# Strassen-Winograd weight sums made by accumulating transfers, with the signs of the products changed

## The chip, the cores and the metric

The kernel runs on one core of a Trainium2 chip. The metric is device time in microseconds of one execution. TensorE (PE) does the matmuls, VectorE (DVE), ScalarE (ACT) and GpSimd (POOL) the elementwise work; SyncE (SP) only issues transfers, and 16 DMA engines carry them.

## The reference

The model is an encoder of depth 2 over 1024 rows of width 1024, in float32. Layer 0 mixes by a Fourier transform and neighbourhood attention, layer 1 by a gated short convolution; after that each layer has a cross-attention into 256 memory rows and a gated feed-forward part:

```python
def conv_ffn(h, w_up, conv_w, conv_b, w_down):
    z = h @ w_up
    u = z[..., :D_FF]
    g = dwconv3_centred(z[..., D_FF:], conv_w) + conv_b
    return (jax.nn.gelu(g, approximate=False) * u) @ w_down

def short_gated_conv_mixer(h, w_in, conv_w, w_out):
    z = h @ w_in
    gate_b = z[..., :D_MODEL]
    gate_c = z[..., D_MODEL:2 * D_MODEL]
    u = z[..., 2 * D_MODEL:]
    return (gate_b * dwconv3_centred(gate_c * u, conv_w)) @ w_out
```

D_FF is 2048, so `w_up` is 1024 by 4096 and `w_down` 2048 by 1024. The change concerns only these weight matrices: `w_up` and `w_down` of both layers, and `w_in` and `w_out` of the gated convolution.

## The kernel before

Activations lie transposed in SBUF, with features in the partitions and the 1024 rows in the free dimension. A float32 matmul is done as three matmuls of halves (`mm3`, L223 to L227): every operand is split into a rounded part *hi* (ACT, L220) and the rest *lo* (DVE, L221; in some other stages POOL), and PE adds hi·hi, hi·lo and lo·hi in PSUM.

The big projections use the Strassen-Winograd scheme: each 2x2 block product takes seven products p1 to p7 of a sum of weight blocks with a sum of activation blocks in place of eight. The weights are handled in *groups*. A group holds four quarters a11, a12, a21, a22, each a tile of 128 partitions by 1024 float32 (512 KB) prepared in that layout by the host, and the seven products need

```
p1: a11    p2: a12 (p2 keeps a12 as it came)    p7: a11 - a21
p6: s2 = a22 - (a11 - a21)    p3: a12 - s2    p5: a21 + a22    p4: a22
```

So four sums are made per group, on DVE: L1069, L1071, L1078 (L1065 where p2 comes late) and L1083. Each result is split (ACT cast, DVE rest) before its product. There are 30 groups: 16 in the two up-projections (u0 and u1, 8 each), 4 of the gated convolution's first projection (c0 to c3, between them four plain blocks b0 to b3), 8 in the two down-projections (d0 and d1, two column couples by two row segments), 2 in the convolution's output projection (oc).

One product of one group is 24 matmuls of 512 columns on 128x128 weights (two output tiles by four contraction tiles by three passes), 168 for the seven. After a product, `post` (L1335 and its like) adds the PSUM bank into the Winograd chains with DVE or ACT: in p1 and p2 ACT copies the bank (L1283, L1288), in the others DVE adds. In the up-projection the finished columns go through the width-3 convolution (L995 on ACT, L996 and L998 on DVE), a gelu and a product, and are stored to DRAM in sums that the down-projection wants (`put`, L1256); the down-projection loads them (`xload`, L1477) and the residual rows h (L1486).

The order is that of the program, on every engine: each engine works through its instructions in the order of issue, and a transfer waits at the head of its issuing queue until its slot in SBUF and its source are ready. SBUF is cut into slots (`p`, 128x1024 float32 in pool 2), handed out by `alloc` and given back by `free`. A list of tasks (loads and preparations of weights) is written by `plan_up`, `plan_conv` and `plan_down`; after each product `ahead(4, ...)` (L1021) emits up to four of the next tasks while enough slots are free, and `until` (L1017) emits what a product needs at once. Groups 0 to 3 do their p1 and p2 first (`wq_early` loads these two weights once more for groups 1 to 3). When an up-projection begins, `xb1` (L1168) makes the activation sums X2 to X7, their splits included, on DVE and ACT beside the first products. All weight loads go out on SP's queue.

## Time and profile before

| what | us |
|---|---|
| median of 3 runs (lowest, highest) | 2244.9 (2243.98, 2247.43) |
| the profiled execution | 2245.92 |
| its span in the trace | 2243.8 |
| PE busy in the span | 2171.9 (97%) |
| DVE busy | 1576.7 (70%) |
| ACT busy | 947.5 (42%) |
| POOL busy | 300.5 (13%) |

The first up-projection runs from about 683 to 1028 us and its tail overlaps the first down-projection (to about 1183), the convolution's first projection follows to 1419, its output projection to 1502, the second cross-attention to 1725, the second up-projection from there to about 2075, and the second down-projection to the end. A busy share is an average over all of these; what an engine waits for is read stage by stage.

### The profile page before, as it was taken

How to read it: one execution, taken by the hardware profiler on the slowest of the kernel's cores; microseconds unless marked ns; L12 is line 12 of the kernel's file. 1: busy time of each engine (PE TensorE's matmuls, PEld its weight loads, DVE VectorE, ACT ScalarE, POOL GpSimd, SP SyncE). 2: the span in 40 equal slices, each digit the busy share in tenths (PEclk: the TensorE clock that was granted, in tenths of full speed). 3: DMA queues.
4: the chain of work that ended last, by engine and by line, in shares of the span. 5: the costliest groups of instructions: out<-in, count | busy, mean ns of one | idle time of the engine just before them, and what ended most of it. 6: DMA issues, size and time to landing. Idle time of an engine off the chain costs nothing.

```text
span 2243.8 us, 26137 instructions
## 1 busy us (share of the span) xinstructions
PE 2171.9 (97%) x10174; PEld 1790.4 (80%) x10174; DVE 1576.7 (70%) x2035; ACT 947.5 (42%) x1362; POOL 300.5 (13%) x140
## 2 busy tenths in 40 slices
PE   8999999999998999999999999999999899999998
PEld 8978888878886778877888888778888677887787
DVE  6764446575657697778867777986555779768884
ACT  6532444254535343434544222545444433424453
POOL 6421223232320000000000000032322000000002
PEclk9999999999999999999999999999999999999999
DMA  9411123132223232346341234523223223325532
GB/s 372 141 64 41 58 64 130 47 104 86 93 104 113 99 139 82 111 176 258 122 138 69 99 127 151 198 83 113 94 72 144 85 93 119 121 91 199 232 122 76
DMA packets 88219, 270.89 MB, mean 121 GB/s; under 512 B 9632, under 2 KB 11936, under 8 KB 88096
## 3 DMA queue, kind: packets, MB, share of 16 engines
q1 hardware_dynamic: 88096, 269.24, 34.2%
q8 instruction: 79, 1.29, 0.2%
q14 instruction: 44, 0.36, 0.1%
HBM read 211.53 MB, written 57.67 MB: 120 GB/s over the span
## 4 chain that ended last, share of the span: by engine, by line
PE 79%; DVE 11%; DMA 6%; issue 2%; ACT 2%; POOL 0%; DVEq 0%; SPq 0%; ACTq 0%
PE PS L227 26%; PE PS L226 26%; PE PS L225 26%; DVE p L221 3%; DVE p L351 1%; DMA xd_d<-p 1%; DMA p<-in_w_up_dram 1%; DMA p<-in_w_down_dram 1%; ACT p L220 1%; DVE p L318 1%; PE PS L922 1%; DVE p L996 1%; DVE p L998 1%; DMA p<-xd_d 1%; DMA xd_oc<-p 0%
## 5 line engine op out<-in xcount | busy, mean ns | idle before, releaser
L225 PE MATMUL PS<-p,p 128*128 128x512 f32 (+1 forms) x3264 | 1230.2, 380 | 29.5 <-ACT p L1283 14.4
L226 PE MATMUL PS<-p,p 128*128 128x512 f32 (+1 forms) x3264 | 1235.9, 379 | 14.1 <-DVE p L221 14.0
L227 PE MATMUL PS<-p,p 128*128 128x512 f32 (+1 forms) x3264 | 1223.3, 379 | 12.6 <-DVE p L221 11.8
L220 ACT CAST p<-p 128x1024 fp32r<-128x1024 f32 (+1 forms) x566 | 529.6, 959 | 590.2 <-PE PS L227 77.1
L225 PEld LDWEIGHTS PS<-p,p 128*128 128x128 f32 x3264 | 618.4, 190 | 156.4 <-ACT p L220 17.0
L227 PEld LDWEIGHTS PS<-p,p 128*128 128x128 f32 x3264 | 619.2, 190 | 136.9 <-DVE p L221 15.8
L226 PEld LDWEIGHTS PS<-p,p 128*128 128x128 f32 x3264 | 619.4, 190 | 136.5 <-DVE p L221 18.4
L221 DVE TENSOR_TENSOR p<-p,p 128x1024 fp32r<-128x1024 f32 (+2 forms) x457 | 503.8, 1122 | 111.1 <-ACT p L220 79.6
L221 POOL TENSOR_TENSOR p<-p,p 128x1024 fp32r<-128x1024 f32 (+1 forms) x109 | 274.2, 2525 | 1333.1 <-ACT p L220 1177.6
L312 ACT ACTIVATE p<-p 128x512 f32<-128x512 f32 (+1 forms) x128 | 74.3, 589 | 133.0 <-DVE p L810 64.0
L318 DVE TENSOR_TENSOR p<-p,p 128x512 f32<-128x512 f32 (+1 forms) x111 | 90.9, 821 | 38.7 <-ACT p L312 36.7
L221 DVE TENSOR_TENSOR p<-PS,p 128x512 fp32r<-128x512 f32 (+3 forms) x92 | 67.7, 744 | 60.5 <-ACT p L220 60.0
L810 DVE TENSOR_TENSOR p<-PS,p 128x512 f32<-128x512 f32 x64 | 44.0, 687 | 72.7 <-PE PS L227 72.4
L1658 POOL TENSOR_TENSOR p<-p,p 128x512 f32<-128x512 f32 (+1 forms) x15 | 16.4, 1123 | 523.3 <-DVE p L492 523.3
L220 ACT CAST p<-PS 128x512 fp32r<-128x512 f32 (+3 forms) x92 | 57.4, 632 | 53.3 <-PE PS L227 30.5
L1069 DVE TENSOR_TENSOR p<-p,p 128x1024 f32<-128x1024 f32 x30 | 36.7, 1222 | 51.6 <-DMA p<-in_w_up_dram 49.8
L995 ACT ACTIVATE p<-p,vec 128x1024 f32<-128x1024 f32 x32 | 39.7, 1245 | 53.7 <-DVE p L1345 47.1
L1288 ACT COPY p<-PS 128x512 f32<-128x512 f32 x40 | 23.5, 586 | 90.5 <-PE PS L227 83.0
L996 DVE SCALAR_TENSOR_TENSOR p<-p,vec,p 128x1023 f32<-128x1023 f32 x40 | 51.1, 1279 | 15.0 <-ACT p L995 15.0
L351 DVE SCALAR_TENSOR_TENSOR p<-p,vec,p 128x512 f32<-128x512 f32 x48 | 52.3, 1120 | 2.6 <-DMA kvd<-p 2.3
L998 DVE SCALAR_TENSOR_TENSOR p<-p,vec,p 128x1023 f32<-128x1023 f32 x40 | 51.0, 1276 | 0.1
L874 DVE SCALAR_TENSOR_TENSOR p<-PS,p 128x512 fp32r<-128x512 f32 x32 | 21.9, 686 | 38.7 <-ACT p L873 38.6
(158 smaller groups left out, 1146.7 us busy)
## 6 DMA issues: line engine op xcount, KB each, us to landing
p<-in_w_up_dram SPq DMA_DIRECT2D x76, 512.0 KB, 3.3
xd_d<-p SPq DMA_DIRECT2D x112, 256.0 KB, 2.6
p<-xd_d SPq DMA_DIRECT2D x56, 512.0 KB, 4.1
p<-in_wq_dram SPq DMA_DIRECT2D x32, 512.0 KB, 3.3
p<-in_wo_dram SPq DMA_DIRECT2D x32, 512.0 KB, 3.3
p<-in_w_down_dram SPq DMA_DIRECT2D x32, 512.0 KB, 7.5
p<-in_w_cc_dram SPq DMA_DIRECT2D x22, 512.0 KB, 3.4
p<-in_xT_dram SPq DMA_DIRECT2D x16, 512.0 KB, 7.0
```

Of the source, the lines that this page charges most:

```text
L220: self.nc.scalar.copy(hi, src)
L221: (eng or self.nc.vector).tensor_tensor(lo, src, hi.bitcast(F32), op=ALU.subtract)
L225: mm(ps, whi, xhi, start=first, stop=False, skip_group_check=True)
L226: mm(ps, whi, xlo, start=False, stop=False, skip_group_check=True)
L227: mm(ps, wlo, xhi, start=False, stop=last, skip_group_check=True)
L312: nc.scalar.activation(t.f(0, w), src, AF.Square)
L318: nc.vector.tensor_tensor(st[ch].f(0, w), st[ch].f(0, w), t.f(0, w), op=ALU.add)
L351: nc.vector.scalar_tensor_tensor(t.f(0, CH), self.hch(k, ch), self.vec[:, gcol + k:gcol + k + 1], y.f(0, CH), op0=ALU.mult, op1=ALU.mult)
L810: self.nc.vector.tensor_tensor(hc, ps, hc, op=ALU.add)
L995: nc.scalar.activation(tmp.f(), src, AF.Identity, scale=v[:, w[1]:w[1] + 1], bias=v[:, bias:bias + 1])
L996: nc.vector.scalar_tensor_tensor(tmp.f(1, S), src[:, 0:S - 1], v[:, w[0]:w[0] + 1], tmp.f(1, S), op0=ALU.mult, op1=ALU.add)
L998: nc.vector.scalar_tensor_tensor(tmp.f(0, S - 1), src[:, 1:S], v[:, w[2]:w[2] + 1], tmp.f(0, S - 1), op0=ALU.mult, op1=ALU.add)
```

## The change

A group's four sums are no longer made by DVE. The seven weights of a group are now loaded into seven slots (`wraw`, on SP), and where a sum is wanted a second transfer, issued from GpSimd with `accum_op=add`, adds another tile to the slot: r7 = a11 + a21 and r5 = a22 + a21 with the second tile from DRAM, r6 = a22 + r7 and r3 = a12 + r6 with the second tile from SBUF. Since these transfers add where DVE subtracted, the signs of the products are changed to fit: the activation sums are taken the other way round in places, and `post` subtracts where it added. That changes operands of DVE instructions, not how many there are.

Per group there are 7 loads in place of 4 (of 4 and 2 early ones in groups 1 to 3 of an up-projection and of the convolution), and 4 accumulating transfers. Over the program the weight loads go from 138 to 210, the accumulating transfers from 0 to 120, and the sums on DVE from 120 to 0; matmuls and splits stay. `plan_couples` now writes the task list of the up-projection and of the convolution, and asks for the three chained sums of the next group after p7 of the one before. `wq_early` now also loads p1 and p2 of group 0, whose splits come from `wload`. The scratch for software-made transfer descriptors grows from 1024 to 4096.

```diff
--- before.py
+++ after.py
                 n -= 1
 
 
-    def wq_load(self, key, quarter, src):
+    def wraw(self, key, p, src):
+        r = self.op[key, "r", p] = yield from self.alloc(F32)
+        self.nc.sync.dma_start(r.f(), src)
+        return r
+
+    def add(self, r, src):
+        self.nc.gpsimd.dma_start(r.f(), src, accum_op=ALU.add)
+
+    def wq_load(self, key, p, src):
+
         def gen():
-            r = yield from self.alloc(F32)
-            self.nc.sync.dma_start(r.f(), src)
-            self.op[key, quarter] = r
-        self.task((key, quarter), 1, gen)
-
-    def wq_prep(self, key, p, ready=None, late=False):
-
-        tt = self.nc.vector.tensor_tensor
-        op = self.op
+            r = yield from self.wraw(key, p, src[{1: 0, 2: 1, 4: 3, 5: 3}[p]])
+            if p == 5:
+                self.add(r, src[2])
+        self.task((key, "r", p), 1, gen)
+
+    def wq_sums(self, key, src):
 
         def gen():
-            def whole(x):
-                hi, lo = yield from self.wide_split(x.f())
-                op[key, p] = (hi.r(), lo.r(), (hi, lo))
-                self.free(x)
-            if p in (1, 2):
-                x = op[key, "11" if p == 1 else "12"]
-                hi, lo = yield from self.wide_split(x.f())
-                op[key, p] = (hi.r(), lo.r(), (hi, lo))
-                if p == 2 and (key, "s2") in op:
-                    s2 = op.pop((key, "s2"))
-                    tt(x.f(), x.f(), s2.f(), op=ALU.subtract)
-                    self.free(s2)
-            elif p == 6:
-                a11, a21, a22 = (op[key, n] for n in ("11", "21", "22"))
-                tt(a11.f(), a11.f(), a21.f(), op=ALU.subtract)
-                s2 = yield from self.alloc(F32)
-                tt(s2.f(), a22.f(), a11.f(), op=ALU.subtract)
-                if late:
-                    hi, lo = yield from self.wide_split(s2.f())
-                    op[key, p] = (hi.r(), lo.r(), (hi, lo))
-                    op[key, "s2"] = s2
-                else:
-                    a12 = op[key, "12"]
-                    tt(a12.f(), a12.f(), s2.f(), op=ALU.subtract)
-                    yield from whole(s2)
-            elif p in (4, 5):
-                if (key, "s1") not in op:
-                    a21 = op[key, "s1"] = op.pop((key, "21"))
-                    tt(a21.f(), a21.f(), op[key, "22"].f(), op=ALU.add)
-                yield from whole(op[key, "22" if p == 4 else "s1"])
-            else:
-                yield from whole(op.pop((key, "11" if p == 7 else "12")))
-        self.task((key, p), 3 if p == 6 else 2, gen, ready)
+            prev = None
+            for p, i in ((7, 0), (6, 3), (3, 1)):
+                r = yield from self.wraw(key, p, src[i])
+                self.add(r, prev.f() if prev else src[2])
+                prev = r
+        self.task((key, "r", 7), 3, gen)
+
+    def wq_prep(self, key, p, ready=None):
+
+        def gen():
+            r = self.op.pop((key, "r", p))
+            hi, lo = yield from self.wide_split(r.f(), self.nc.vector)
+            self.op[key, p] = (hi.r(), lo.r(), (hi, lo))
+            self.free(r)
+        self.task((key, p), 2, gen, ready)
 
     def wq_early(self, key, p, src):
...
             t1 = self.raw[1, m]
-            tt(t1.f(), r.f(), t1.f(), op=ALU.subtract)
+            tt(t1.f(), t1.f(), r.f(), op=ALU.subtract)
             r = yield from self.alloc(F32)
...
             x = yield from self.alloc(F32)
-            tt(x.f(), r.f(), t1.f(), op=ALU.subtract)
+            tt(x.f(), r.f(), t1.f(), op=ALU.add)
...
-        tt(t1, b12, b11, op=ALU.subtract)
-        tt(t2, b22, t1, op=ALU.subtract)
+        tt(t1, b11, b12, op=ALU.subtract)
+        tt(t2, b22, t1, op=ALU.add)
         self.put(tag, s, k, 6, t2)
-        tt(t3, b22, b12, op=ALU.subtract)
+        tt(t3, b12, b22, op=ALU.subtract)
...
                 nc.scalar.copy(g[q].f(0, U), u[q].f(U, 2 * U))
-            nc.vector.tensor_tensor(u[q].f(U, 2 * U), b, g[q].f(0, U), op=ALU.add)
+            nc.vector.tensor_tensor(u[q].f(U, 2 * U), b, g[q].f(0, U), op=ALU.subtract)
 
 
...
-        def load(c, quarters=(0, 1, 2, 3)):
-            for i in quarters:
-                self.wq_load(keys[c], QUARTERS[i], src[c, i])
-
-        def prep(c, ps):
+        self.plan_couples(keys, src)
+
+    def plan_couples(self, keys, src, between=None):
+
+        def load(c, *ps):
             for p in ps:
-                self.wq_prep(keys[c], p)
+                self.wq_load(keys[c], p, src[c])
 
         def early(c, p):
-            self.wq_early(keys[c], p, src[c, p - 1])
-        load(0, (0,))
-        prep(0, (1,))
+            self.wq_early(keys[c], p, src[c][p - 1])
+        early(0, 1)
         early(1, 1)
-        load(0, (1,))
-        prep(0, (2,))
+        early(0, 2)
         early(1, 2)
+        self.wq_sums(keys[0], src[0])
         early(2, 1)
         early(3, 1)
         early(2, 2)
         early(3, 2)
-        load(0, (2, 3))
         self.wq_prep(keys[0], 6, lambda: len(self.X.get(6, ())) == 2)
-        for c in range(8):
-            prep(c, (7,) if c == 0 else (6, 7) if c < 4 else (1, 2, 6, 7))
-            if c < 7:
-                load(c + 1)
-            prep(c, (5, 4, 3))
+        n = len(keys)
+        for c, key in enumerate(keys):
+            if c > 3:
+                self.wq_prep(key, 1)
+            if c > 0:
+                self.wq_prep(key, 6)
+            if c > 3:
+                self.wq_prep(key, 2)
+            load(c, 5, 4)
+            self.wq_prep(key, 7)
+            if c < n - 1:
+                self.wq_sums(keys[c + 1], src[c + 1])
+            self.wq_prep(key, 5)
+            if 2 < c < n - 1:
+                load(c + 1, 1, 2)
+            self.wq_prep(key, 4)
+            if between:
+                between(c, 0)
+            self.wq_prep(key, 3)
+            if between:
+                between(c, 1)
 
...
-                tt(g[q].f(U, 2 * U), b, g[q].f(0, U), op=ALU.add)
+                tt(g[q].f(U, 2 * U), b, g[q].f(0, U), op=ALU.subtract)
             elif p == 5:
-                tt(g[q].f(U, 2 * U), b, g[q].f(U, 2 * U), op=ALU.add)
+                tt(g[q].f(U, 2 * U), g[q].f(U, 2 * U), b, op=ALU.subtract)
             elif p == 4:
-                tt(g[q].f(0, U), b, g[q].f(0, U), op=ALU.add)
+                tt(g[q].f(0, U), b, g[q].f(0, U), op=ALU.subtract)
                 t = o[q] = yield from self.alloc(F32)
                 self.conv3(t, g[q].f(), [FCONV_W + (l * 3 + j) * 16 + i for j in range(3)], FCONV_B + l * 16 + i)
                 self.free(g[q])
...
-        early("c2", 2)
-        early("c3", 2)
-        load("c0", (2, 3))
-        self.wq_prep("c0", 6, lambda: len(self.X.get(6, ())) == 2)
-        for i, n in enumerate(seq):
-            prep(n, (7,) if i == 0 else (6, 7) if n[0] == "c" else (1, 2, 6, 7))
-            if i < 7:
-                load(seq[i + 1])
-            prep(n, (5, 4, 3))
+                for p in PREP:
+                    self.w1_prep(n, p)
+        self.plan_couples(["c%d" % k for k in range(4)], cc, single)
 
...
@@ -1465,10 +1444,13 @@
 
 
     def plan_down(self, tag, segs, src):
-        def load(s, *quarters):
-            for i in quarters:
+        def load(s, *ps):
+            for p in ps:
                 for c in range(2):
-                    self.wq_load((tag, c, s), QUARTERS[i], src[c, s, i])
+                    if p == 7:
+                        self.wq_sums((tag, c, s), src[c, s])
+                    else:
+                        self.wq_load((tag, c, s), p, src[c, s])
 
         def xload(s, p):
             for m in range(2):
 
         def prep(p, s):
             for c in range(2):
-                self.wq_prep((tag, c, s), p, None, p == 6 and s == 0 and segs == 2)
+                self.wq_prep((tag, c, s), p)
 
         def rows():
             for k in (4, 5, 6, 7, 0, 1, 2, 3):
                 row(k)
 
-        load(0, 0)
+        load(0, 1)
         if segs == 2:
             xload(0, 1)
+            load(0, 7)
             prep(1, 0)
-            load(0, 2, 3)
+            load(1, 1)
             xload(0, 6)
             prep(6, 0)
-            load(1, 0)
+            load(0, 2)
             prep(1, 1)
             rows()
             xload(1, 1)
-            load(0, 1)
+            load(1, 2)
             xload(0, 2)
             prep(2, 0)
-            load(1, 1, 2, 3)
+            load(1, 7)
             n = 4
         else:
+            load(0, 2)
             prep(1, 0)
-            load(0, 1)
+            load(0, 7)
             prep(2, 0)
             rows()
-            load(0, 2, 3)
             xload(0, 1)
             xload(0, 2)
             n = 2
-        for p, s in self.down_order(segs)[n:]:
+        order = self.down_order(segs)
+        for i, (p, s) in enumerate(order[n:]):
             xload(s, p)
+            if p == 7:
+                load(s, 4)
+            if p == 4:
+                load(s, 5)
             prep(p, s)
 
     @staticmethod
...
@@ -1808,7 +1796,7 @@
 
     data = prepare(**{n: np.asarray(a) for n, a in inputs.items()})
     nc = _bacc.Bacc("TRN2", target_bir_lowering=False, num_devices=1,
-                    dynamic_dma_scratch_size=1024)
+                    dynamic_dma_scratch_size=4096)
     arrays, ap = {}, {}
     for n, a in data.items():
         arrays[f"in_{n}_dram"] = a
```

How the rows move is shown at three places; in these rows `p_43_5309` is an SBUF tile, number 43 of its pool, with the number of its use.

The first is DVE at the start of the first up-projection, where X4 (L1200 before, L1188 after), weight sums (L1071, L1083, L1078) and splits (L221) stand one after another. Before:

```order
643 L1200 TENSOR_TENSOR p_43_5309<-p_43_5309,p_37_5620 128x1024
644 L1071 TENSOR_TENSOR p_10_5918<-p_12_5773,p_46_5564 128x1024
645 L1083 TENSOR_TENSOR p_31_5771<-p_31_5771,p_12_5773 128x1024
646 L221 TENSOR_TENSOR p_51_5760<-p_26_5302,p_7_5759 128x1024
647 L221 TENSOR_TENSOR p_6_5624<-p_37_5620,p_11_5623 128x1024
648 L221 TENSOR_TENSOR p_22_5697<-p_5_5605,p_30_5696 128x1024
649 L1200 TENSOR_TENSOR p_14_5316<-p_14_5316,p_8_5642 128x1024
650 L221 TENSOR_TENSOR p_19_5646<-p_8_5642,p_21_5645 128x1024
651 L221 TENSOR_TENSOR p_50_5702<-p_29_5627,p_17_5701 128x1024
652 L221 TENSOR_TENSOR p_36_5926<-p_46_5564,p_41_5925 128x1024
653 L1078 TENSOR_TENSOR p_27_5655<-p_27_5655,p_10_5918 128x1024
654 L221 TENSOR_TENSOR p_2_5764<-p_43_5309,p_40_5763 128x1024
```

After:

```order
642 L1188 TENSOR_TENSOR p_43_5309<-p_43_5309,p_37_5620 128x1024
643 L221 TENSOR_TENSOR p_6_5624<-p_37_5620,p_11_5623 128x1024
644 L1188 TENSOR_TENSOR p_14_5316<-p_14_5316,p_8_5642 128x1024
645 L221 TENSOR_TENSOR p_31_5706<-p_5_5605,p_50_5705 128x1024
646 L221 TENSOR_TENSOR p_19_5646<-p_8_5642,p_21_5645 128x1024
647 L221 TENSOR_TENSOR p_46_5711<-p_29_5627,p_36_5710 128x1024
648 L221 TENSOR_TENSOR p_5_5773<-p_43_5309,p_2_5772 128x1024
649 L221 TENSOR_TENSOR p_8_5735<-p_15_5732,p_28_5734 128x1024
650 L221 TENSOR_TENSOR p_0_5729<-p_37_5726,p_20_5728 128x1024
651 L221 TENSOR_TENSOR p_45_5777<-p_14_5316,p_29_5776 128x1024
```

The three weight sums among the rows of before are gone, and the splits of the activation sums and of early weights follow directly.

The second is POOL, after its last split for the cross-attention, in the same up-projection. Before, POOL does no work between 690 us and the end of the gated convolution's first projection. After:

```order
96 L1048 DMA p_47_5667<-in_w_up_dram 128x1024
97 L1048 DMA p_48_5670<-p_47_5667 128x1024
98 L1048 DMA p_30_5673<-p_48_5670 128x1024
99 L1048 DMA p_9_5900<-in_w_up_dram 128x1024
100 L1048 DMA p_3_5991<-in_w_up_dram 128x1024
101 L1048 DMA p_20_5994<-p_3_5991 128x1024
102 L1048 DMA p_0_5997<-p_20_5994 128x1024
103 L1048 DMA p_24_6128<-in_w_up_dram 128x1024
```

The first three are group 0's r7, r6 and r3 in their chain, then its r5; then the same for group 1: four a group, in order, each with its source behind the arrow.

The third is SP at the start of the first down-projection: L1256 (L1244 after) stores product columns to `xd`, L1477 (L1459) loads an activation tile, L1045 (L1044) loads weights. The names are `xd_d_` segment, product, pair, half. Before:

```order
268 L1256 DMA xd_d_1_5_1_7487<-p_51_7794 128x512
269 L1045 DMA p_36_7957<-in_w_down_dram 128x1024
270 L1045 DMA p_39_7959<-in_w_down_dram 128x1024
271 L1256 DMA xd_d_1_2_1_7445<-p_37_7539 128x512
272 L1256 DMA xd_d_1_3_1_7489<-p_37_7539 128x512
273 L1477 DMA p_3_7845<-xd_d_1_1_1_7424 128x1024
274 L1256 DMA xd_d_1_6_1_7479<-p_51_7794 128x512
275 L1256 DMA xd_d_1_7_1_7482<-p_47_7795 128x512
276 L1045 DMA p_0_7851<-in_w_down_dram 128x1024
```

After:

```order
293 L1244 DMA xd_d_1_1_1_7452<-p_38_7556 128x512
294 L1044 DMA p_30_7887<-in_w_down_dram 128x1024
295 L1244 DMA xd_d_1_5_1_7524<-p_51_7830 128x512
296 L1244 DMA xd_d_1_7_1_7519<-p_40_7831 128x512
297 L1244 DMA xd_d_1_6_1_7516<-p_51_7830 128x512
298 L1244 DMA xd_d_1_4_1_7522<-p_40_7831 128x512
299 L1459 DMA p_8_7921<-xd_d_0_2_1_6484 128x1024
300 L1459 DMA p_28_8021<-xd_d_1_6_0_6991 128x1024
301 L1044 DMA p_2_8139<-in_w_down_dram 128x1024
302 L1459 DMA p_29_7881<-xd_d_1_1_1_7452 128x1024
303 L1459 DMA p_51_7915<-xd_d_0_2_0_6074 128x1024
```

The load of `xd_d_1_1_1` (the second half of the activations of p1 in segment 1) stood directly behind stores; now it stands directly behind a weight load, `p_2_8139` (p4 of segment 0), which takes over the slot of the first half's rounded part and so waits until the first half of that same product has been read.

## Rows read from the trace of the kernel before

**Rows 1.** The page: busy time of TensorE, and the hardware DMA queue.
```profile
PE 2171.9 (97%) x10174; PEld 1790.4 (80%) x10174; DVE 1576.7 (70%) x2035; ACT 947.5 (42%) x1362; POOL 300.5 (13%) x140
...
q1 hardware_dynamic: 88096, 269.24, 34.2%
```

**Rows 2.** Waits of TensorE: engine, its line, releaser; total us, times, longest.
```profile
PE PS L225 <- ACT p L1283: 14.4, 4, 6.8
PE PS L226 <- DVE p L221: 14.0, 9, 3.0
PE PS L225 <- ACT p L220: 12.8, 8, 3.3
PE PS L227 <- DVE p L221: 11.8, 7, 2.7
```

**Rows 3.** Instructions by line: one of DVE's weight sums; busy, mean ns, idle before.
```profile
L1083 DVE TENSOR_TENSOR p<-p,p 128x1024 f32<-128x1024 f32 x30 | 36.4, 1220 | 1.0 <-issue 0.4
```

**Rows 4.** Timeline of TensorE, three starts after a wait: start us, duration; [idle].
```profile
727.54 0.80 PE L225 MATMUL PS<-p,p 128*128 128x512 f32 x1 [6.65 <-ACT p L1283]
...
770.79 0.50 PE L227 MATMUL PS<-p,p 128*128 128x512 f32 x1 [2.46 <-DVE p L221]
...
772.18 0.63 PE L226 MATMUL PS<-p,p 128*128 128x512 f32 x1
...
814.05 0.50 PE L227 MATMUL PS<-p,p 128*128 128x512 f32 x1 [2.75 <-DVE p L221]
```

**Rows 5.** Timeline of DVE, first up-projection.
```profile
714.29 1.22 DVE L1071 TENSOR_TENSOR p<-p,p 128x1024 f32<-128x1024 f32 x1
715.43 1.22 DVE L1083 TENSOR_TENSOR p<-p,p 128x1024 f32<-128x1024 f32 x1
...
724.51 1.22 DVE L1078 TENSOR_TENSOR p<-p,p 128x1024 f32<-128x1024 f32 x1
```

**Rows 6.** Timeline of ScalarE, the same place.
```profile
726.90 0.59 ACT L1283 COPY p<-PS 128x512 f32<-128x512 f32 x1 [1.23 <-DVE p L221]
```

**Rows 7.** Busy us of engines in stretches, then clock, DMA share, GB/s.
```profile
720.00:850.00 130.00, 117.84 (x491) 93.92 (x490) 104.44 (x119) 46.55 (x50) 0.00 (x0) 0.96 0.29 104
850.00:985.00 135.00, 135.00 (x584) 109.37 (x584) 101.18 (x115) 48.58 (x51) 0.00 (x0) 1.00 0.30 100
960.00:1060.00 100.00, 91.10 (x376) 72.50 (x375) 81.37 (x87) 39.87 (x42) 0.00 (x0) 0.95 0.61 227
1180.00:1400.00 220.00, 220.00 (x953) 178.44 (x953) 174.00 (x216) 74.35 (x99) 0.00 (x0) 1.00 0.31 110
1420.00:1510.00 90.00, 86.86 (x365) 68.93 (x364) 80.94 (x93) 40.58 (x50) 20.27 (x8) 0.98 0.37 124
1770.00:1900.00 130.00, 118.64 (x491) 93.98 (x490) 103.72 (x117) 46.06 (x49) 0.00 (x0) 0.95 0.31 104
```

**Rows 8.** Waits of TensorE, second up-projection, 1765 to 1870 us.
```profile
PE PS L225 <- ACT p L1283: 7.3, 2, 6.8
PE PS L227 <- DVE p L221: 2.9, 2, 2.5
PE PS L225 <- DVE p L1293: 1.4, 2, 1.0
```

**Rows 9.** Waits of TensorE, start of the first down-projection, 980 to 1060 us.
```profile
PE PS L225 <- ACT p L220: 5.7, 2, 3.3
PE PS L226 <- DVE p L221: 2.9, 1, 2.9
```

**Rows 10.** Timeline of ScalarE, the same place.
```profile
1048.30 1.04 ACT L220 CAST p<-p 128x1024 fp32r<-128x1024 f32 x1 [4.88 <-DMA p<-in_w_down_dram]
```

**Rows 11.** The page: DMA issues, KB each, median us to landing.
```profile
p<-in_w_up_dram SPq DMA_DIRECT2D x76, 512.0 KB, 3.3
```

**Rows 12.** DMA issues of 960 to 1060 us.
```profile
p<-in_w_down_dram SPq DMA_DIRECT2D x16, 512.0 KB, 7.5
p<-xd_d SPq DMA_DIRECT2D x13, 512.0 KB, 7.2
```

More of the change, by code (lines that the diff above doesn't have):

```diff
@@ L1113, in gen @@
             if p == 6:
-                tt(a11, a11, a21, op=ALU.subtract)
+                tt(a11, a11, a21, op=ALU.add)
                 s2 = yield from self.alloc(F32, 1)
-                tt(s2.f(0, U), a22, a11, op=ALU.subtract)
-                tt(a12, a12, s2.f(0, U), op=ALU.subtract)
+                tt(s2.f(0, U), a22, a11, op=ALU.add)
+                tt(a12, a12, s2.f(0, U), op=ALU.add)
                 src = s2.f(0, U)
@@ L1352, in post @@
             else:
-                tt(u[q].f(U, 2 * U), b, u[q].f(U, 2 * U), op=ALU.add)
+                tt(u[q].f(U, 2 * U), b, u[q].f(U, 2 * U), op=ALU.subtract)
                 tt(u[q].f(U, 2 * U), u[q].f(U, 2 * U), o[q].f(U, 2 * U), op=ALU.mult)
@@ L1369, in plan_conv, with single @@
         cc, cb = self.ap["w_cc"], self.ap["w_cb"]
[L1371 to L1402 removed]
+        def single(c, part):
+            n = "b%d" % c
+            if part == 0:
+                for i in range(2):
+                    self.w1_load(n, i, cb[c, i])
+            else:
+                for p in PREP:
+                    self.w1_prep(n, p)
+        self.plan_couples(["c%d" % k for k in range(4)], cc, single)
     def conv_post(self, n, tag):
@@ L1453, in outer @@
             else:
-                tt(u[0].f(0, U), b, u[0].f(0, U), op=ALU.add)
+                tt(u[0].f(0, U), b, u[0].f(0, U), op=ALU.subtract)
                 tt(ga.f(U, 2 * U), ga.f(U, 2 * U), u[0].f(0, U), op=ALU.mult)
@@ L1549, in post @@
                 nc.scalar.copy(t1.f(0, U), b)
-                tt(self.hch(j, 0), self.hch(j, 0), t1.f(0, U), op=ALU.add)
+                tt(self.hch(j, 0), self.hch(j, 0), t1.f(0, U), op=ALU.subtract)
             elif p == 6:
                 t2 = yield from self.alloc(F32, 1)
-                tt(t2.f(0, U), b, t1s[c, q].f(0, U), op=ALU.add)
-                tt(self.hch(i, 1), self.hch(i, 1), t2.f(0, U), op=ALU.add)
+                tt(t2.f(0, U), b, t1s[c, q].f(0, U), op=ALU.subtract)
+                tt(self.hch(i, 1), self.hch(i, 1), t2.f(0, U), op=ALU.subtract)
                 self.free(t2)
@@ L1557, in post @@
                 t1 = t1s.pop((c, q))
-                tt(t1.f(0, U), b, t1.f(0, U), op=ALU.add)
+                tt(t1.f(0, U), b, t1.f(0, U), op=ALU.subtract)
                 tt(self.hch(j, 1), self.hch(j, 1), t1.f(0, U), op=ALU.add)
@@ L1567, in post @@
                 x = self.h[k].f(CH + a, CH + a + n)
-                tt(x, b, x, op=ALU.add)
+                tt(x, x, b, op=ALU.subtract if p == 5 else ALU.add)
                 if fin is None:
```

38 lines of the change are left out of this document (9 added, 29 removed).

## The prediction

> **What bounds the kernel now.** I read the busy row of the page first: PE is busy 97% of the span, so only the 72 us in which it isn't, and the time it runs at a low clock, can be won; the 146 us of sums that leave DVE are no gain by themselves [rows 1, 3]. Next the waits of PE by releaser: four pairs hold 53.0 us, always a split or an opening copy on ACT or DVE that comes late [rows 2]. The timeline places them. In the first up-projection there is one gap of 6.65 us where PE waits for ACT's copy of the last opening product, and two of 2.46 and 2.75 us where it waits for a split on DVE [rows 4]. The second up-projection repeats it with 7.3 us for the copy, 2.9 us for the split and 1.4 us for a sum of an opening product [rows 8]. The start of the first down-projection loses 5.7 and 2.9 us to splits [rows 9]. After such a gap the matmuls' rows grow longer (0.63 us at 772.18 [rows 4]): for some microseconds TensorE is granted the lower of its two levels, 1.2 in place of 2.4 GHz, so that the granted clock is 0.96 over 720 to 850 and 1.00 over 850 to 985, where no gap lies [rows 7]. In that later stretch, and in the convolution's first projection, PE is busy without a break [rows 7]: there DVE's sums cost nothing today.
>
> **What goes from DVE.** 30 instructions each on L1069, L1071 and L1083, and 30 on L1078 and L1065 together, at 1220 ns: 120 x 1.22 = 146 us [rows 3]. Over 850 to 985 DVE is busy 101 of 135 us, with PE at 135 of 135, so these sums are hidden there [rows 7]. Only the two up-projection starts, the down starts and the convolution's output can give something back.
>
> Up start, layer 0, the copy gap. The copy stands at 726.90 on ACT, behind splits that follow DVE's order [rows 6]. On DVE two sums stand at 714.29 and 715.43 and a third at 724.51, beside which X4 and its splits are made [rows 5]; a sum takes the row on for 1.14 us (714.29 to 715.43), three 3.4 us. The new order has none of them there, and the splits of the activation sums come up. So I shorten the gap of 6.65 by 3.4 us; what is late next is X4 and its splits, which stay.
>
> The split gaps, 2.46 + 2.75 = 5.2 us, go to a queue on DVE that holds the four sums of group 1 (4 x 1.14 = 4.6 us); each gap is shorter than that, so both close. The clock loss over 720 to 850 is 130 x (1 - 0.96) = 5.2 us [rows 7]; two of three gaps close, the smaller two, and I count a third of it, 1.7 us. Layer 0: 3.4 + 5.2 + 1.7 = 10.3 us.
>
> Layer 1: 3.4 of the 7.3 us, the 2.9 and 1.4 us in full [rows 8], and a third of 130 x (1 - 0.95) = 6.5 us [rows 7], 2.2: 9.9 us. Together 20.2 us. The bounds: nothing, if the copy waits for the activation sums anyway and the splits for weights, and 6.65 + 5.2 + 5.2 + 7.3 + 4.3 + 6.5 = 35 us, if all goes. The value between is by the DVE rows.
>
> **What comes to the queues.** A 512 KB load costs the 16 DMA engines 34.2% x 2243.8 us / 269.24 MB x 0.524 MB = 1.49 us of their time [rows 1]. No row shows an accumulating transfer. From below it costs what a load does, 1.49 us (less is excluded, since it writes as many bytes and reads no fewer); from above I take 6 us, four loads' worth, with nothing in the trace against it. I take 3.0, twice a load, since it must read what it adds to as well as what it adds, so the nearest row counts twice. The Trainium skill (Collectives: The Full Stack, The bandwidth ceiling: the fold count and why AG ≠ RS ≠ AR) says that an add inside a transfer is slow not by the adding but because it needs two reads of source per write, and halves the rate; no run here shows that yet; by it the cost is the 3.0 us too, and by a plain copy's rule the 1.49 us, at which nothing below fills up.
>
> In the up-projections a group of 168 matmuls takes 168 x 135.00 / 584 = 38.8 us, and DMA is busy 0.30 of it, 11.6 us [rows 7]. Three more loads (4.5 us) and four accumulating ones (12 us) make 28 us, 72%: it fits. In sequence the four are issued one after another on POOL's queue, and each chained one waits for the one before it to land, so each may take 38.8 / 4 = 9.7 us; a load takes 3.3 us there [rows 11], twice that is 6.6. They are asked for four to nine products ahead of use (22 to 50 us at 5.55 us per product, 24 x 0.231), so they are hidden at 6.6 us and their cost is zero. If that cover goes, PE waits for the split of p6, and behind the split stand ACT's convolution activations. The bounds are 0 and, at 11 us each, (11 - 9.7) x 4 = 5.2 us per group. By the Trainium skill's DMA: Bandwidth & Descriptors (Anatomy of one DMA) a transfer has some 2 us of fixed cost beside its bytes, which as an estimate makes the chain of three about 13 us; the trace's 3.3 us for a load agrees with its size.
>
> **The down starts.** Here DMA is the crowded resource: over 960 to 1060 its share is 0.61, 61 us of 100 [rows 7], and transfers take 7.5 and 7.2 us in place of 3.3 [rows 11, 12]. Before, all 16 weight loads of the four groups lie there [rows 12]. After, some 22 loads lie there (p1, p2, p7, p6 and p3 of each group and the first p4), 6 more, 9 us, and 12 accumulating transfers (the chains of four groups), 36 us at 3.0: 106 of 100. At 1.49 us it would be 88. So at 3.0 us the start is just full, and what is late is pushed into the stretch behind it.
>
> The one wait I can place is X of p1 in segment 1: its second half now stands on SP behind a weight load that waits for the first half's products. Its load (7.2 us [rows 12]) and cast (1.05 us, as the one at 1048.30 [rows 10]) then come after, while PE has four matmuls, 0.9 us, left: 7.2 + 1.05 - 0.9 = 7.4 us of gap against the 2.4 + 2.9 = 5.3 us of today (5.7 less its longest wait of 3.3, which is that of segment 0, and 2.9 [rows 9]). That is +2.1 us per start, +4 for two. Queued behind that load on SP are the other activation loads of the start, and PE's products of p2 wait for those. The bounds are -8 us per start (both waits go, with the sums that stood ahead of the splits) and +23 (below).
>
> **The rest.** Convolution, first projection: PE has no gap [rows 7], so 0, unless its weights come late. Its output: PE is idle 3.1 us of 90 and loses 90 x 0.02 = 1.8 us by clock [rows 7]; two groups change there, between -4.9 and, by the same measure, +4.9: 0. The subtractions for additions in `post` cost what they cost before. Sum: -20.2 + 4 + 0 = -16.2; from the profiled execution of 2245.9 that is 2229.7. It lay 1.0 us over the median of the runs, so 2229.
>
> **Rivals.** *Saturated down starts (slower).* If an accumulating transfer costs the engines 4 us, the start wants 61 + 9 + 48 = 118 us of 100: 18 us late, with another 5 us of low clock as in that stretch today (clock 0.95 or so), 23 us per start. 2244.9 - 20.2 + 46 = 2271. It turns the sign where two starts lose more than 20.2, 10.1 each: 70 + 12a - 100 = 10.1, a = 3.3 us, just over my value. For it: the share of 1.0 in the present peak and the 7.5 us loads. Against it: some of that traffic can move past 1060, and the groups are asked for eight products ahead.
>
> *Chains too slow everywhere (slower).* If the four in order take more than 9.7 us each, every group is late: at 11 us, 5.2 us x 22 groups outside the down-projections = 114, so 2339. For it: software-made descriptors on a queue that no row of this trace shows. Against it: loads of the same size take 3.3 us.
>
> *No change.* The up starts win little, because the copy gap is set by X4 and its splits, or the down starts give back what is won: 2244 (2241 to 2248).
>
> *All waits go.* Up starts 35 us and half of the down waits with their clock, (8.6 + 5) x 2 / 2 = 14: 2244.9 - 49 = 2196. For it: all these waits end in splits that share DVE with the sums. Against it: both copy gaps also have ACT's own splits ahead.
>
> *The sums don't leave DVE.* The order shows 120 rows fewer on DVE, so I give that nothing.
>
> **How the numbers follow.** Forecast, 2215 to 2240: 0.40. All waits go: 0.15. No change: 0.14. Saturated down starts: 0.22. Slow chains: 0.09. A measurement of this kernel tells about 0.2%, 4.5 us, from no change. Faster is 0.40 + 0.15 = 0.55, the same 0.14, slower 0.31. The range leaves out the slow chains and the far ends of the two beside: 2196 to 2280.
>
> **What would show it.** Right: no L1069 to L1083 on DVE; the wait for the copy at 3 to 4 us in each up start and the two split waits gone; the granted clock over the up starts above 0.97; accumulating transfers landing in 5 to 7 us in the up-projections; DMA share about 0.7 there and near 1.0 in the down starts, with a gap of about 7 us for p1 of segment 1. Wrong: PE waiting in the steady part of an up-projection or in the convolution (slow chains); down starts that lose more than 10 us beyond today (saturated); or copy gaps of unchanged size.

## The result and the profile after

The changed kernel takes 2325.8 us (median of 4 runs, 2319.3 to 2328.3) against 2245.7 for the one before: a ratio of 1.0352, interval 1.0329 to 1.0375. Its profiled span is 2324.5 us, 80.7 more. The prediction was 2229 us, faster, in a range of 2196 to 2280: wrong in sign and size.

The page of the kernel after, against [rows 1]: busy time of PE and DVE, and the DMA queues, now two.

```profile
PE 2192.7 (94%) x10174; PEld 1799.0 (77%) x10174; DVE 1441.6 (62%) x1915; ACT 943.7 (41%) x1362; POOL 404.3 (17%) x260
...
q1 hardware_dynamic: 98464, 306.99, 37.1%
q0 software_dynamic: 17280, 62.92, 14.7%
```

DVE is busy 135 us less, near the 146 expected. PE is busy 21 us more, though its matmuls are the same, because more of them ran at the low clock: the mean granted clock is 0.973 in place of 0.985. The other 60 of the 80.7 us are time in which PE stands idle (131.8 us in place of 71.9). The software-made queue is new: 14.7% of 2324.5 us for 120 transfers is 2.85 us each.

The waits of PE after, against [rows 2]: releaser, total us, times, longest.

```profile
PE PS L225 <- ACT p L220: 76.9, 23, 11.2
PE PS L226 <- DVE p L221: 9.8, 10, 2.4
PE PS L225 <- DVE p L1281: 7.8, 2, 4.5
PE PS L227 <- DVE p L221: 7.4, 8, 3.2
```

One row has taken the lead: the wait for a cast on ACT, 12.8 us before, 76.9 now. The waits for splits on DVE went from 14.0 and 11.8 to 9.8 and 7.4.

The stretches after, against [rows 7] (where the kernel has shifted, the stretch that answers to the one of before): busy time of PE, PEld, DVE, ACT, POOL, then clock, DMA share and GB/s.

```profile
720.00:850.00 130.00, 118.17 (x483) 93.17 (x483) 84.23 (x98) 47.04 (x50) 12.99 (x15) 0.96 0.69 191
850.00:985.00 135.00, 125.27 (x520) 100.33 (x519) 75.84 (x90) 41.97 (x45) 11.99 (x14) 0.96 0.68 193
960.00:1060.00 100.00, 93.31 (x386) 74.45 (x385) 62.30 (x73) 36.75 (x39) 10.41 (x12) 0.95 0.91 273
1205.00:1430.00 225.00, 217.90 (x932) 175.25 (x931) 155.22 (x203) 75.42 (x100) 12.71 (x15) 0.98 0.48 135
1450.00:1555.00 105.00, 87.32 (x357) 69.54 (x356) 74.50 (x85) 43.39 (x53) 23.14 (x14) 0.92 0.63 201
1820.00:1950.00 130.00, 118.13 (x484) 93.24 (x484) 85.15 (x99) 49.04 (x53) 13.02 (x15) 0.96 0.69 192
```

In every stretch the DMA share is up (from 0.29 and 0.30 to 0.69 and 0.68 in the first up-projection), and PE, which was busy without a break over 850 to 985 and in the convolution, now has holes there. The loss isn't at one place. The first matmul of each stage, found by the order of the matmuls in the trace, gives how long each stage took in the span (us, to within some 2 us):

| stage | before | after | no adds | idle adds | short adds |
|---|---|---|---|---|---|
| first up-projection, to the first product of the down | 312.2 | 323.5 | 298.2 | 311.9 | 307.5 |
| first down-projection, to the convolution | 184.3 | 196.9 | 183.0 | 198.2 | 185.3 |
| convolution's first projection | 230.0 | 243.7 | 235.0 | 236.4 | 235.0 |
| its output and the cross-attention | 315.1 | 328.2 | 310.4 | 326.0 | 314.4 |
| second up-projection, to the end of group 6 | 302.4 | 316.1 | 297.0 | 308.6 | 302.3 |
| from there to the end of the down-projection | 203.6 | 218.7 | 196.1 | 212.1 | 200.2 |

(The last three columns are experiments, below, each from one profiled execution; that of the short adds took 2241.2 us, 7 less than the median of its runs.) Each stage lost 11 to 15 us.

The transfers after, against [rows 11, 12]: KB each, median us from issue to landing.

```profile
p<-in_w_up_dram SPq DMA_DIRECT2D x112, 512.0 KB, 4.8
p<-p POOLq DMA_DIRECT2D x60, 512.0 KB, 6.4
xd_d<-p SPq DMA_DIRECT2D x112, 256.0 KB, 5.7
...
p<-xd_d SPq DMA_DIRECT2D x56, 512.0 KB, 6.6
...
p<-in_w_up_dram POOLq DMA_DIRECT2D x32, 512.0 KB, 7.3
```

A weight load lands in 4.8 us in place of 3.3, and the stores and loads of the activation sums (2.6 and 4.1 us before, on the page) take 5.7 and 6.6. An accumulating transfer takes 6.4 (from SBUF) or 7.3 us (from DRAM).

How that becomes a wait of PE can be followed in the steady part of the first up-projection. SP, then POOL, then ACT, then PE there; a row is start, duration, engine, line, operands and in brackets the idle time before it with its releaser.

```profile
906.85 2.13 SPq L1044 DMA_DIRECT2D p<-in_w_up_dram  x3
```

```profile
914.72 0.87 POOL L1048 DMA_DIRECT2D p<-in_w_up_dram  x1 [21.67 <-DVE p L1352]
921.66 0.86 POOL L1048 DMA_DIRECT2D p<-p  x1 [6.07 <-DMA xd_d<-p]
```

```profile
929.90 1.04 ACT L220 CAST p<-p 128x1024 fp32r<-128x1024 f32 x1 [8.48 <-DMA p<-p]
930.85 0.58 ACT L1274 COPY p<-PS 128x512 f32<-128x512 f32 x1
```

```profile
931.49 0.50 PE L225 MATMUL PS<-p,p 128*128 128x512 f32 x1 [1.85 <-ACT p L1274]
```

SP issues weight loads from 906.85 on; by the trace's landing times the third of them, issued at 907.78, landed at 914.08. The adds follow at 914.72, 0.6 us after that landing, and at 921.66, 0.5 us after the first add landed (by these times the adds waited for these two, and not for the releasers in POOL's brackets). The second add landed at 929.83 and ends the wait of 8.48 us of ACT's cast at 929.90. Behind that cast stands the copy of an opening product at 930.85, for which PE waits 1.85 us. So some 22 us pass from the load to the cast, in a place where the old kernel needed a load and a few sums of 1.2 us.

### The profile page after: what moved, and what is told of

Its sections match the earlier page's. It is cut to its first block, busy times and chain, and to the rows that moved or that the text cites. A ratio compares the mean times of both kernels' runs of the same rounds, so it can differ in the third digit from the quotient of the medians.

```text
span 2324.5 us, 26634 instructions
## 1 busy us (share of the span) xinstructions
PE 2192.7 (94%) x10174; PEld 1799.0 (77%) x10174; DVE 1441.6 (62%) x1915; ACT 943.7 (41%) x1362; POOL 404.3 (17%) x260
## 3 DMA queue, kind: packets, MB, share of 16 engines
q0 software_dynamic: 17280, 62.92, 14.7%
## 5 line engine op out<-in xcount | busy, mean ns | idle before, releaser
L225 PE MATMUL PS<-p,p 128*128 128x512 f32 (+1 forms) x3264 | 1242.2, 384 | 97.5 <-ACT p L220 76.9
L226 PE MATMUL PS<-p,p 128*128 128x512 f32 (+1 forms) x3264 | 1240.1, 380 | 9.9 <-DVE p L221 9.8
L227 PE MATMUL PS<-p,p 128*128 128x512 f32 (+1 forms) x3264 | 1228.3, 380 | 8.1 <-DVE p L221 7.4
L226 PEld LDWEIGHTS PS<-p,p 128*128 128x128 f32 x3264 | 622.8, 191 | 133.4 <-DVE p L221 15.9
L227 PEld LDWEIGHTS PS<-p,p 128*128 128x128 f32 x3264 | 621.0, 190 | 133.9 <-DVE p L221 12.6
L221 DVE TENSOR_TENSOR p<-p,p 128x1024 fp32r<-128x1024 f32 (+2 forms) x457 | 505.9, 1125 | 275.3 <-ACT p L220 233.3
L221 POOL TENSOR_TENSOR p<-p,p 128x1024 fp32r<-128x1024 f32 (+1 forms) x109 | 273.8, 2521 | 539.6 <-ACT p L220 347.1
L1048 POOL DMA_DIRECT2D p<-p x60 | 51.9, 864 | 417.5 <-DMA p<-p 77.9
L318 DVE TENSOR_TENSOR p<-p,p 128x512 f32<-128x512 f32 (+1 forms) x111 | 92.4, 834 | 40.9 <-ACT p L312 38.9
L221 DVE TENSOR_TENSOR p<-PS,p 128x512 fp32r<-128x512 f32 (+3 forms) x92 | 67.6, 744 | 60.0 <-ACT p L220 59.4
L1048 POOL DMA_DIRECT2D p<-in_w_up_dram x32 | 29.2, 911 | 389.1 <-DMA p<-in_w_up_dram 149.1
L810 DVE TENSOR_TENSOR p<-PS,p 128x512 f32<-128x512 f32 x64 | 43.9, 687 | 72.3 <-PE PS L227 72.3
L1281 DVE TENSOR_TENSOR p<-PS,p 128x512 f32<-128x512 f32 x40 | 27.5, 687 | 65.2 <-ACT p L1274 48.1
```

The costliest lines, as they stand in the source:

```text
L221: (eng or self.nc.vector).tensor_tensor(lo, src, hi.bitcast(F32), op=ALU.subtract)
L225: mm(ps, whi, xhi, start=first, stop=False, skip_group_check=True)
L226: mm(ps, whi, xlo, start=False, stop=False, skip_group_check=True)
L227: mm(ps, wlo, xhi, start=False, stop=last, skip_group_check=True)
L318: nc.vector.tensor_tensor(st[ch].f(0, w), st[ch].f(0, w), t.f(0, w), op=ALU.add)
L810: self.nc.vector.tensor_tensor(hc, ps, hc, op=ALU.add)
```

## Experiments

What was to be told apart: *A*, the wait for the adds, counted from when a slot comes free; *B*, the traffic of the adds, which makes all other transfers late; *C*, the new order, signs and slots, whoever adds. The kernel before took 2243.1 us when the first four of these runs were made (no adds, sums on DVE, plain copies, adds without the chain) and 2246.4 to 2247.3 with the others, so a difference between a run of the first four and one of the others is uncertain by some 4 us.

**No adds.** The transfers are left out, and with them the sums.

```diff
     def add(self, r, src):
-        self.nc.gpsimd.dma_start(r.f(), src, accum_op=ALU.add)
+        pass
```

> The changed kernel with the 120 accumulating transfers left out, and nothing in their place: the sums are not made, r7, r6, r3 and r5 hold one quarter each. Theories A and B: 2215 to 2240 us, below the kernel before, since neither DVE nor the queues make the sums. Rival C: 2290 or more.

2216.5 us, ratio to before 0.988 (0.986 to 0.991). Its waits of PE and its transfers:

```profile
PE PS L225 <- ACT p L220: 19.9, 15, 3.7
```

```profile
p<-in_w_up_dram SPq DMA_DIRECT2D x112, 512.0 KB, 3.8
xd_d<-p SPq DMA_DIRECT2D x112, 256.0 KB, 4.1
...
p<-xd_d SPq DMA_DIRECT2D x56, 512.0 KB, 4.5
```

So C falls: the new order with its 72 more loads, but without adds, is 27 us faster than before, and the 120 adds cost 2325.8 - 2216.5 = 109 us.

**Sums on DVE in the new order.** The tile a21 is loaded into an eighth slot.

```diff
-                self.add(r, prev.f() if prev else src[2])
...
+            if p == 6:
+                for d, s in ((7, 21), (6, 7), (3, 6)):
+                    d, s = op[key, "r", d].f(), op[key, "r", s].f()
+                    tt(d, d, s, op=ALU.add)
```

> The changed kernel with its new order, signs and task list, but a21 loaded into an eighth slot by a plain transfer and the four sums made in place on DVE just before the split of p6 (r7, r6, r3) and of p5. No accumulating transfer is left; loads per group go from 7 to 8. Theory A (latency: load, then accumulating transfers of about 7 us each in a chain, counted from the moment a slot comes free, make p6's split late, and ACT and PE wait behind it): back to 2225 to 2245 us, since DVE's sums take 1.2 us each. Theory B (load on the 16 DMA engines: 120 x 2.85 us more): also back, 2230 to 2250. Rival C (more slots and loads, or the new order of the splits, whoever adds): stays at 2290 to 2320.

2260.7 us, ratio 1.0074 (1.0055 to 1.0092). Of the changed kernel's 80 us most is gone, but the time lies above both expectations and 44 us above the version without sums. Its waits of PE are casts and opening copies again:

```profile
PE PS L225 <- ACT p L220: 21.9, 11, 5.7
PE PS L225 <- ACT p L1279: 13.4, 4, 5.3
```

Three sums now stand in one piece ahead of p6's split, and a group holds eight slots. How the 44 us divide between these was not tried.

**Plain copies in place of adds.** Same queue, same chain, overwriting; the sums are left out.

```diff
-        self.nc.gpsimd.dma_start(r.f(), src, accum_op=ALU.add)
+        self.nc.gpsimd.dma_start(r.f(), src)
```

> The same transfers on GpSimd's queue in the same chain, but plain copies that overwrite in place of adding: the sums are not made. Theory A: what counts is the serial latency; a copy by this queue lands in about 4.5 us in place of 7, so about 60% of the 80 us stays, 2275 to 2300 us. Theory B: a copy costs the DMA engines half of an add, so more than half goes, 2240 to 2270. If the software-made queue itself is the cost: unchanged, 2310 to 2325.

2278.2 us, ratio 1.0146 (1.0124 to 1.0168). Queue and landing times:

```profile
q0 software_dynamic: 17280, 62.92, 7.4%
```

```profile
p<-p POOLq DMA_DIRECT2D x60, 512.0 KB, 4.0
...
p<-in_w_up_dram POOLq DMA_DIRECT2D x32, 512.0 KB, 5.4
```

A copy takes 7.4% x 2277.0 / 120 = 1.40 us of the 16 engines, an add 2.85: twice, as the prediction took it, and as the Trainium skill has it for the adds of a reduction between cores (Collectives: The Full Stack, The bandwidth ceiling: the fold count and why AG ≠ RS ≠ AR). The time lies in theory A's range, near its lower end, and 8 us above theory B's. By itself that doesn't part the two, since a copy both lands sooner and takes half of the DMA time.

**Adds without the chain.** r6 and r3 add a21 from DRAM, so two sums are others than wanted.

```diff
-                self.add(r, prev.f() if prev else src[2])
+                self.add(r, src[2])
```

> All 120 accumulating transfers stay, but those of r6 and r3 add a21 from DRAM in place of r7 and r6, so none waits for another to land (two of the seven weights are then other sums than wanted). Theory A: most of the loss goes, 2250 to 2280 us, since p6's weight is ready one load and one accumulation after its slot in place of two accumulations. Theory B: same bytes and more of them from DRAM, 2315 to 2335.

2303.9 us, ratio 1.0264 (1.0247 to 1.0282): without the chain 22 of the 109 us are gone, net of what reading a21 from DRAM costs in place of a tile in SBUF. The time lies between the two ranges, so neither theory alone gave this.

**Idle adds.** The traffic without the wait: each add goes from the loaded tile to a scratch tile in DRAM (the sums are left out).

```diff
+        self.nadd += 1
+        s = self.scr[self.nadd % 2]
+        if self.nadd <= 2:
+            self.nc.gpsimd.dma_start(s, r.f())
+        else:
+            self.nc.gpsimd.dma_start(s, r.f(), accum_op=ALU.add)
```

> The changed kernel, but each of the 120 accumulating transfers adds the tile that was just loaded to one of two scratch tiles in DRAM, and nobody waits for it (the sums are left out). The DMA engines keep about the added traffic, while no split waits for an add. The version without the transfers took 2216, the changed kernel 2326. Theory A (it is the wait for the adds, counted from when a slot comes free): 2216 to 2240. Theory B (it is the traffic, which makes every other load and store land later): 2290 to 2330.

2290.4 us, ratio 1.0189 (1.0174 to 1.0205). Queue, transfers, and ACT's waits for the scratch transfers (lines here are 2 higher):

```profile
q0 software_dynamic: 17280, 62.92, 15.3%
...
scr<-p POOLq DMA_DIRECT2D x120, 512.0 KB, 7.6
p<-in_w_up_dram SPq DMA_DIRECT2D x112, 512.0 KB, 5.1
xd_d<-p SPq DMA_DIRECT2D x112, 256.0 KB, 5.9
...
p<-xd_d SPq DMA_DIRECT2D x56, 512.0 KB, 7.2
```

```profile
ACT p L222 <- DMA scr<-p: 18.9, 4, 4.9
```

74 of the 109 us stay though no sum is waited for. Loads, stores and activation loads land as late as in the changed kernel (5.1, 5.9 and 7.2 us). It isn't wholly idle: a transfer that is still reading holds its tile's slot, and ACT waited 18.9 us for such (SP's loads 17.8 us); how much of the 74 that makes was not parted. What ACT waits for longer than in the version without adds is above all the loads of activation sums, here in that version and in this one:

```profile
ACT p L220 <- DMA p<-xd_d: 64.3, 34, 5.9
...
ACT p L220 <- DMA p<-in_w_up_dram: 53.8, 25, 5.3
```

```profile
ACT p L222 <- DMA p<-xd_d: 88.8, 40, 8.2
...
ACT p L222 <- DMA p<-in_w_up_dram: 56.6, 23, 5.7
```

Its waits for weight loads of the up-projections hardly grew, though these loads land 1.3 us later.

**Idle copies.** The same with half of the traffic.

```diff
-            self.nc.gpsimd.dma_start(s, r.f(), accum_op=ALU.add)
+            self.nc.gpsimd.dma_start(s, r.f())
```

> As the run with idle traffic (2290 us), but plain copies to the scratch tiles in DRAM in place of adds, so about half of the DMA time (a copy by this queue took 1.40 us of the 16 engines, an add 2.85); nobody waits for them, the sums are left out. If the loss grows with the traffic in proportion: 2216 + 74 / 2 = 2253 (2245 to 2262). If it begins only where the DMA engines are full: 2216 to 2232. If the queue and not the bytes holds things up: above 2275.

2250.3 us, ratio 1.0014 (1.0003 to 1.0025). Its queue and transfers:

```profile
q0 software_dynamic: 17280, 62.92, 7.1%
...
p<-in_w_up_dram SPq DMA_DIRECT2D x112, 512.0 KB, 4.2
```

The loss is 34 us for 7.1% x 2245.7 = 159 us of DMA time, and 74 us for 15.3% x 2288.2 = 350: 0.21 us per us both times. These two and the version without lie on a line within the 4 us; nothing here shows a share below which traffic is free, and three points don't show that there is none.

**Short adds.** The waits without the traffic: the chain stays, each add takes 64 of 1024 columns (the rest of the sums is left out).

```diff
-        self.nc.gpsimd.dma_start(r.f(), src, accum_op=ALU.add)
+        self.nc.gpsimd.dma_start(r.f(0, 64), src[:, 0:64], accum_op=ALU.add)
```

> The changed kernel with all its accumulating transfers in their chain and order, but each adds only 64 of the 1024 columns (the rest of the sums is left out): the waits, the queue and the order stay, one sixteenth of the bytes remains. Theory B: 2216 to 2225. Theory A in the form that the fixed latency of a transfer counts: such an add lands in some 2.5 us in place of 7, a third of the 109 us stays, 2245 to 2260. If GpSimd's queue itself holds things up: above 2280.

2248.0 us, ratio 1.0004 (0.9995 to 1.0014): 32 us above the version without adds. Its queue, and ACT's wait for these adds:

```profile
q0 software_dynamic: 17280, 3.94, 2.0%
```

```profile
ACT p L220 <- DMA p<-p: 45.7, 13, 7.1
```

So A and B are both true, B for about two thirds. (The short adds still take 2.0% x 2239.4 = 45 us of DMA time; at 0.21 us per us some 9 of the 32 us would be traffic.) The parts nearly add up: 74 (idle adds) + 32 (short adds) = 106 of 109; and 34 (idle copies) + 32 = 66 against 62 for the copies that are waited for.

**Asking earlier.** The reserves of free slots are lowered, so that the same transfers are asked for sooner.

```diff
-KEEP = 8
-KEEPD = 6
+KEEP = 5
+KEEPD = 4
```

> The changed kernel with the two reserves of free slots, below which no task is emitted ahead, lowered from 8 and 6 to 5 and 4, so loads and sums are asked for earlier. If the lead in the program's order is what is short (theory A): some of the third that waiting costs comes back, 2290 to 2315. If traffic, or slots that come free late, set the time: 2315 to 2335.

2360.9 us, ratio 1.0499 (1.0481 to 1.0517): worse by 35 us. The waits of PE moved from casts to the copies of opening products (before this edit 76.9 and 6.3 us):

```profile
PE PS L225 <- ACT p L220: 43.8, 15, 13.7
PE PS L225 <- ACT p L1274: 27.7, 10, 6.1
```

Asking earlier took 33 us from PE's waits for casts and cost more elsewhere. ACT's opening copies now stand waiting for stores to land, 40.9 us in place of 10.6:

```profile
ACT p L1274 <- DMA xd_d<-p: 40.9, 7, 8.1
```

Such a copy writes to a slot that `alloc` hands out; with a smaller reserve it seems to get one more often that a store is still reading. That this makes up the 35 us isn't shown; PE's waits for splits on DVE (L227, 7.4 to 17.9 us) and for DVE's L1281 (7.8 to 17.0) grew as well.

**Half of the sums by transfer.** The four slots and loads of before; DVE makes r7 and r6, transfers from SBUF make r5 and r3.

```diff
-                tt(a11.f(), a11.f(), a21.f(), op=ALU.subtract)
+                tt(a11.f(), a11.f(), a21.f(), op=ALU.add)
+                op[key, "s1"] = op.pop((key, "21"))
+                self.nc.gpsimd.dma_start(a21.f(), a22.f(), accum_op=ALU.add)
...
-                    tt(a12.f(), a12.f(), s2.f(), op=ALU.subtract)
+                    self.nc.gpsimd.dma_start(a12.f(), s2.f(), accum_op=ALU.add)
```

> A version that takes from both: the four slots, four loads and task list of the kernel before, the signs of the changed one; r7 and r6, which are wanted soon, are summed on DVE, and r5 and r3, which are wanted later, by an accumulating transfer from SBUF issued as soon as DVE has made what they need. 60 accumulating transfers in place of 120 and no more loads than before. If an accumulating transfer costs nothing where it has time (theory A): 2225 to 2242, by 60 fewer sums on DVE. If the traffic counts (theory B): 60 x 2.85 us more of DMA time, 2250 to 2275.

2251.0 us, ratio 1.0021 (1.0011 to 1.0030), at the lower end of theory B's range: no gain, though no cast of ACT waits for these adds. PE's longest wait is for splits on DVE (L226), 25.9 us in place of 14.0. The full 0.21 us per us would be 35 us (its queue's share was 7.4%, so 60 x 2.77 us x 0.21); whether the 60 sums taken from DVE gave back most of that, or the rate doesn't hold here, wasn't tried.

**Adds only at the starts.** Accumulating transfers for groups 0 and 1 of each up-projection, all else as before (with the signs of the changed kernel).

```diff
+        ACC = 2
+        def prep(c, ps, ready=None):
+            for p in ps:
+                (self.aq_prep if c < ACC else self.wq_prep)(keys[c], p, ready)
...
+            if c < ACC:
+                self.aq_sums(keys[c], src[c])
```

> The kernel before with the signs of the changed one, and accumulating transfers only for groups 0 and 1 of each up-projection, where DVE's queue makes PE wait; all other groups are summed on DVE from four loads as before. 16 accumulating transfers in place of 120. The trace of the changed kernel was 6 us ahead of the one before at the end of group 1 in both up-projections, and lost it later. Theory (gain at the start real, loss elsewhere from traffic and waits): 2245 - 12 = 2233 (2228 to 2240). If the gain of the start is only put off: 2240 to 2250.

2233.5 us, ratio 0.9941 (0.9929 to 0.9953): faster than both kernels, as expected. The starts also take over the new order of loads and splits for these groups, and what order and adds each give wasn't parted. In its first up start PE's waits are:

```profile
PE PS L225 <- ACT p L220: 3.1, 2, 2.5
PE PS L227 <- DVE p L221: 1.8, 1, 1.8
```

**One group.** The same with `ACC = 1`.

> The same with group 0 alone on accumulating transfers, 8 in all. The copy gap, where DVE holds the sums of group 0, is shortened; the two split gaps behind the sums of group 1 stay: about -7 us by the 3.4 us per start and its clock, 2238 (2234 to 2244). If the two are one effect: as with two groups.

2236.2 us, ratio 0.9951 (0.9939 to 0.9963). Its interval overlaps that of two groups; most of the gain is group 0's.

## Why the prediction was wrong

*The up starts, -20.2 us: right in kind, a little too large, and not where I put them.* The waits of PE over 700 to 800 us after:

```profile
PE PS L225 <- ACT p L220: 5.5, 2, 3.0
...
PE PS L225 <- ACT p L1271: 0.7, 1, 0.7
```

The copy gap of 6.65 us is 0.7 now (L1271), which is more than the 3.4 taken off; in its place a cast is waited for, 5.5 us in two waits. Of the two split gaps (5.2 us) 0.6 us is left over 700 to 850. The granted clock over 720 to 850 is 0.96 as before, so the clock term won nothing there. Counted matmul by matmul the changed kernel was at most 8.2 us ahead of the one before in the first up-projection and 8.3 us in the second, 16.5 of the 20.2, and had lost the lead some 40 us later. In the version without adds the first up-projection took 14.0 us less than before and the second 5.4 (the table), together 19.4, though those are whole stages and not the starts alone. With two groups the kernel kept 14 of them.

*The cost of an add: right.* Taken as 3.0 us of the engines, measured 2.85; landing taken as 6.6 us, measured 6.4 to 7.3; the DMA share of the up-projection taken as 72%, measured 68%. The other estimate, about 13 us for the chain of three, was too short: three medians make 7.3 + 6.4 + 6.4 = 20 us.

*"So they are hidden at 6.6 us and their cost is zero": this step failed*, and with it the zeros for the convolution (13.7 us lost) and for its output (13.1 us, the cross-attention included). It drew from a share under 1 and from an order that asks for the sums 22 to 50 us early that nothing waits. Both halves are refuted. Traffic of sums that nobody waits for cost 74 us at a share of 0.72, where the other transfers of these stages land later and ACT was already waiting for some of them; and waiting for the adds cost some 32 us (short adds), because a task stands early in the order but its load starts only when its slot comes free. The group of DVE's first sum on the page of before hinted at it, and I read past it, since PE didn't wait there. As a wait (DVE's line, releaser, total, times, longest), and beside it SP's wait to issue weight loads in the kernel after:

```profile
DVE p L1069 <- DMA p<-in_w_up_dram: 49.8, 13, 10.2
```

```profile
SPq L1044 <- PE PS L227: 304.3, 55, 25.5
```

In 13 of the 16 groups of the up-projections DVE's first sum stood waiting for a weight load, 49.8 us in all: the loads landed after DVE had come to them, so there was little lead to spend. And SP's weight loads stood waiting 55 times for PE to have done with what the slot held. In the steady part shown above the load went out 22 us before the cast that used its sum, and a load and two adds filled all of that.

*The down starts, +2 per start: right in place, too small, and not by the named load alone.* PE's wait for activations came at the predicted place; PE, then the ACT cast that ended it, then SP:

```profile
1077.58 1.22 PE L225 MATMUL PS<-p,p 128*128 128x512 f32 x2 [11.24 <-ACT p L220]
```

```profile
1076.48 1.04 ACT L220 CAST p<-p 128x1024 fp32r<-128x1024 f32 x1 [2.13 <-DMA p<-xd_d]
```

```profile
1067.49 0.69 SPq L1044 DMA_DIRECT2D p<-in_w_down_dram  x1
1069.06 10.06 SPq L1459 DMA_DIRECT2D p<-xd_d  x4
```

It is 11.24 us where 7.4 was taken and 5.3 stood before. The cast at 1076.48 is of a load that SP issued at 1066.85, ahead of the weight load at 1067.49, and that landed at 1076.46. The load that the prediction names stands behind that weight load: issued at 1069.06, it landed at 1079.03, and the next matmul that waited for a cast started at 1080.15. So two loads were late, each taking 9.6 to 10.0 us in place of 7.2. The DMA share over 960 to 1060 is 0.91; the stage lost 12.6 us.

*The rivals.* The time came near the slow chains' 2339, but not by their mechanism: the adds took 6.4 to 7.3 us on the median, not over 9.7, and without the chain the kernel still took 2303.9 us. The sign named for it, PE waiting in the steady part, did come (125.27 of 135 us busy over 850 to 985), and so did that of the saturated down starts (more than 10 us lost there): the signs told where time is lost, not why. Saturated down starts had the right sort of cause, traffic, but confined it to places where the share is near 1. No rival said that traffic costs time at a share of 0.7, wherever engines already wait for transfers; that was the missing one.

## What to carry over

Moving work from an engine with slack to the DMA engines wasn't free here at a DMA share of 0.6 to 0.7: first look for engines that wait for transfers, on any engine and not only on the bounding one. If they do, price each added microsecond of transfer time (here 0.21 us per us, by two runs) and the latency from the moment the destination slot comes free, not from the place in the program. Then use the transfer only where the relieved engine really holds up the bound one, here the first two groups of eight in each up-projection, where the first alone gave most of it.

## What the runs showed of the hardware

An accumulating transfer of 512 KB took 2.85 us of the 16 engines, a copy by the same queue 1.40, a ratio of 2.0. Its landing took 6.4 us from SBUF and 7.3 from DRAM, where copies, in the run with plain copies, took 4.0 and 5.4. Traffic issued by GpSimd slowed the transfers issued by SP (weight loads from 3.8 to 5.1 us, stores from 4.1 to 5.9, between the version without adds and the one with idle adds). That agrees with the Trainium skill, by which transfers run on the same 16 DMA engines and interleave there, whichever engine issued them (DMA: Bandwidth & Descriptors, Issuing engines are not separate DMA queues).
